# A sparse attention stage played from a written list instead of by due times, with three more score tiles and two more probability tiles

## The chip, the core and the metric

The kernel runs on one core of a Trainium2 chip. The metric is the device time of one execution in microseconds: 1283.05 us, the median of 3 runs (1282.41 to 1285.9). The engines are TensorE (PE in the profile; its weight loads are PEld), VectorE (DVE), ScalarE (ACT), GpSimd (POOL) and SyncE (SP), which only issues transfers. Each engine takes its own instructions in order and waits on semaphores for the others.

## What is computed

A convolution and pooling block, then a two-layer transformer on 256 tokens of width 1024, everything in float32. The first layer's mixer is a sparse attention with 16 query heads of 64 on 4 key/value heads, and this is the stage that the change rewrites:

```python
q, kc, vc, ks, vs, kw, vw, gates = split(h @ w_in)
kc = rmsnorm(compress_blocks(kc)); vc = compress_blocks(vc)     # 15 blocks: gelu(block @ w1) @ w2
ks, kw = rmsnorm(ks), rmsnorm(kw)
o_cmp = softmax(q @ kc, alibi, causal) @ vc
o_sel = softmax(q @ ks[selected], alibi, causal) @ vs           # at 256 tokens every block is selected
o_win = softmax(q @ kw, alibi, window) @ vw
o = g0 * o_cmp + g1 * o_sel + g2 * o_win
x = x + o @ w_out
```

Around it lie feed-forward layers (1024 to 2 x 2816 to 1024) and, later, a differential attention layer.

## The kernel before

Activations lie transposed, 128 features on partitions by 256 tokens. A float32 product is made of three fast products: each weight block is split into a rounded part `hi` (ScalarE, line 161) and a rest `lo` (VectorE, line 166), the activations likewise, and `mm3` (line 189) adds hi x hi, hi x lo and lo x hi. Weight blocks of 1 MB come through a ring of 4 `raw` tiles; `hi` and `lo` have 3 tiles each, so a block can be split only when a tile of an earlier block has been read for the last time. `Stream.prep` makes the two halves of each split as separate pieces of work, two blocks ahead. A `raw` tile is free when its `lo` is made, and SyncE then issues the next load.

The sparse stage (`nsa`, line 1035) runs from 430.3 to 596.8 us. Its parts, with the names of the changed text:

- `kc`, `vc`: 48 matmuls of 256 columns each; `post_c` (line 1062) scales them into `c2` (part of the big tile `nsaA`) and GpSimd's queue copies rows between partition halves; `fill_kcp` (F) adds the positions, `w1_q` multiplies with the two halves of the hidden layer (`hid`), `gelu`, `hid_t`, `ktilde_a`, `ktilde_b` (E0 to E3) make the compressed keys and values.
- Four projections of 48 matmuls with 512 columns: `nk`, `nq0`, `nv`, `nq1`, each 8 quanta of 6 matmuls; `norm_tok` (line 921) follows with a square and sum, a chain of twelve small VectorE operations (`factors`), a scaling, and two groups of four transposes (K, Z, N). `gt` is the gate projection, 24 matmuls.
- 16 pair units (4 head groups g, 2 branches b, 2 pairs i), each of seven steps. S: scores of two heads, 8 matmul records on 64 rows each, so that the two heads use different halves of the array. M: bias and running maximum (VectorE). X: exponential (ScalarE). G: reciprocal, gate and scaling (VectorE). T and U: three transposes each, of the first and the second head, and a copy (ScalarE). V: the product with the values, 8 records on 64 columns each, the two heads again on different halves. S takes both PSUM banks `s`, T one bank `pt`, U one bank `ptb`.
- Per group the compressed branch: a and b (softmax), c (transposes), e (product), and v, the evacuation of the group's output `O` into `oh` and `ol`.
- The output projection: 16 quanta of 12 matmuls of 256 columns, `q41` to `q52` and `y0` to `y3` in the new text; `post_res` adds to x and splits x anew (R), `squares` makes the norm's sums (Q).

Up to now the stage gives each piece of work a place in the program with `step`, `run` and `weave`; the units go in with `pipeline` as urgent background. A planner orders each engine's instructions by priority and by when it thinks an operand is ready, so instructions of several steps can mix on an engine. `in_order(True)` (line 339) makes TensorE, VectorE and ScalarE keep the order of the text, as is already done in the differential layer from 970.7 us on. The `P` tiles that hold scores are 5 in all, the `PT` tiles that hold transposed probabilities 3.

Of the kernel before, what the change touches and what calls it, by code (L numbers as in the profile page):

```python
# [17 lines left out]
T = 256  # L18
# [31 lines left out]
ET = mybir.EngineType  # L50
MAN = {ET.PE, ET.DVE, ET.Activation}

ADA_AT = {("win", 6): [(0, 8, 1)], ("win", 7): [(0, 9, 0)], ("win", 8): [(0, 10, 0)], ("win", 10): [(0, 11, 0), (1, 0, 1)],
# [118 lines left out]


PHASES = ("first", 0, "nsa", 1, 2, "diff", 3)


@with_exitstack
def body(ctx: ExitStack, tc, d, out, phases=PHASES):
# [139 lines left out]
    LA = 2  # L318
# [28 lines left out]
    def step(key, quanta, post, pre=(), extra_bg=(), keep=False):  # L347

        i = sid[key] if key is not None else None
        preps = st.prep(st.ahead(i, LA)) if i is not None else ([], [])  # L350
        pend = list(state["pend"])
        extra_bg = [urgent(f) for f in extra_bg]
        run(quanta, pre, weave(preps, pend + list(extra_bg)))
        state["pend"] = list(post)
# [599 lines left out]

        return [a, b, c, e(0), e(1)]

    def tr_unit(u, bank=None):
        def f():
            p = p_pt("PT") if bank is None else bank
            for i in range(3):  # L960
                PE.transpose(p[:, i * 128:(i + 1) * 128], u["s"][:, i * 128:(i + 1) * 128], C("ident"))
            s_ = sb.tile([128, 384], F32, tag="PT", name="PTs", bufs=3)

            A.copy(s_, p[:, 0:384])
            u["pt"] = s_
        return f
# [68 lines left out]
    def nsa():  # L1035
# [131 lines left out]

        def q_dst(g):
            return lambda p: A.copy(qhat[g], p)

        def group(key, post, ahead=False, bg0=(), bg1=()):
            pv = [pmm(key + "0"), pmm(key + "1")]
            step((key, 0), tok_quanta(pv, (key, 0), 0, ahead), [], extra_bg=bg0)
            step((key, 1), tok_quanta(pv, (key, 1), 1), post(pv), extra_bg=bg1)

        def post_v(pv):
            def f():
# [25 lines left out]
        dl = []  # L1203
        def post_nk(pv):
            f = norm_tok(pv, None, [k_dst(0), k_dst(1)], "nk")
            dl.extend(f[3:])
            return f[:3]
        group("nk", post_nk)
        step(("gt",), [gt_q], [post_gt, post_gt2])
        step(("w1", 1), w1_q(0), dl)  # L1210
        group("nq0", lambda pv: norm_tok(pv, C("invs")[:, 0:8], [q_dst(0), q_dst(1)], "nq0"))
        step(("w1", 3), w1_q(1), [gelu, hid_t, ktilde_a, ktilde_b])
        group("nv", post_v)

        obank = {}

# [4 lines left out]
        def cmp_units(g):  # L1221
# [45 lines left out]

            return b, b1, b2, c, e

        def pair_unit(g, i, b, cmp_b):  # L1270

            us = [{}, {}]
            slopes = [NSLOPE[(2 * i + n) * 4 + g] for n in range(2)]
            W = (slice(0, 128), slice(128, 384))
            c0 = 16 if b == 0 else 0
            WS = ((0, 128 + c0), (128 + c0, 384 + 2 * c0))
            kk = ksel if b == 0 else kwin
            qo = i * 256

            def S():  # L1280
                for u in us:
                    u["p"] = p_s("S")
                for t_, (s0, s1) in enumerate(WS):
                    for n, u in enumerate(us):
                        pa = slice(n * 64, n * 64 + 64)
                        mm(u["p"][:, s0:s1], qhat[g][pa, qo + t_ * 128:qo + (t_ + 1) * 128],
                           kk[pa, i, 0:s1 - s0], True, True)

            def M():
                mx = tiny("mx", 4)  # L1290
                nb = C("nbias")
                if b == 0:
                    if i == 0:
                        cell["sc", g] = cmp_b(us)
                    cb = C("cbias").rearrange("p (t n) -> p t n", t=2)
                    for n, u in enumerate(us):
                        V.tensor_tensor(cell["sc", g][:, :, 2 * i + n],
                                        u["p"][:, 0:288].rearrange("p (t n) -> p t n", t=2)[:, :, 0:15], cb, op=ALU.add)
                for n, u in enumerate(us):
                    u["s"] = sb.tile([128, 384], F32, tag="P", name="P", bufs=5)  # L1300
                    for t_, w in enumerate(W):
                        ws = slice(WS[t_][0] + c0, WS[t_][1])
                        V.tensor_tensor_reduce(out=u["s"][:, w], in0=u["p"][:, ws], in1=nb[:, w], scale=1.0,
                                               scalar=-3e38, op0=ALU.add, op1=ALU.max,
                                               accum_out=mx[:, 2 * n + t_:2 * n + t_ + 1])
                nm_ = tiny("nm", 4)
                o = (g * 2 + i) * 4
                V.tensor_tensor(nm_, mx, C("nsl4")[:, o:o + 4], op=ALU.mult)
                us[0]["nm"] = nm_

            def X():
                l = tiny("l", 4)
                for n, u in enumerate(us):
                    for t_, w in enumerate(W):
                        q = 2 * n + t_
                        A.activation(u["s"][:, w], u["s"][:, w], AF.Exp, bias=us[0]["nm"][:, q:q + 1],
                                     scale=slopes[n], accum_out=l[:, q:q + 1])
                us[0]["l"] = l

            def G():  # L1320
                rc = tiny("rc", 4)
                V.reciprocal(rc, us[0]["l"])
                rv = rc.rearrange("p (n t) -> p n t", n=2)
                gv = gts.rearrange("p (t kv g b) -> p kv t g b", t=2, kv=4, g=4)[:, 2 * i:2 * i + 2, :, g, 1 + b]
                V.tensor_tensor(rv, rv, gv, op=ALU.mult)
                for n, u in enumerate(us):
                    for t_, w in enumerate(W):
                        V.tensor_scalar(u["s"][:, w], u["s"][:, w], rc[:, 2 * n + t_:2 * n + t_ + 1], None, op0=ALU.mult)

            def Tr():  # L1330
                if "ptb" not in cell:
                    cell["ptb"] = pmm("ptb")
                for u, bank in zip(us, (None, cell["ptb"])):
                    tr_unit(u, bank)()

            def Av():
                if i == 0 and b == 0:
                    obank[g] = p_o("O")
                o = obank[g]
                vo = b * 256 + i * 128  # L1340
                for kb in range(2):
                    for n, u in enumerate(us):
                        mm(o[n * 64:(n + 1) * 64, i * 256 + kb * 128:(i + 1) * 256],
                           vv[:, kb * 512 + vo + n * 64:kb * 512 + vo + (n + 1) * 64],
                           u["pt"][:, 0:256] if kb == 0 else u["pt"][:, 256:384],
                           i == 0 and b == 0 and kb == 0, kb == 1)

            return {"S": S, "M": M, "X": X, "G": G, "T": Tr, "V": Av}

        def evac(g):  # L1350
            def f():
# [8 lines left out]
        seq = {g: [] for g in range(4)}  # L1360
        mark = {}
        for s_, sl in enumerate(slots):
            g, r = s_ // 4, s_ % 4
            lst = seq[min(g, 3)]
            lst += sl
            if g < 4 and r == 1:
                lst.append(cmps[g][1])
            elif g < 4 and r == 2:
                lst += [cmps[g][2], cmps[g][3]]
            if r == 2 and g >= 1:  # L1370
                lst += [cmps[g - 1][4], evac(g - 1)]
                mark.setdefault(g, len(lst))
        group("nq1", lambda pv: norm_tok(pv, C("invs")[:, 8:16], [q_dst(2), q_dst(3)], "nq1"),
              bg0=seq[0][:len(seq[0]) // 2], bg1=seq[0][len(seq[0]) // 2:])
        pend_, state["pend"] = state["pend"], []
        run([], (), weave(([], pend_), seq[1]))
        cut = mark[3]
        c_ = range(3)
        out_proj("no", oh, ol, P("ffn2")[:, 0:8],
                 [([(j, 0) for j in c_], 1, seq[2], ()), ([(j, 1) for j in c_], 2, seq[3][:cut], ()),  # L1380
                  ([(j, 2) for j in c_], 3, seq[3][cut:], ()), ([(0, 3)], 0, (), (0,)), ([(1, 3)], 4, (), (1,)),
                  ([(2, 3)], 0, (), (2,)), ([(3, ch) for ch in range(4)], 5, (), (3,))])


    def diff():
# [385 lines left out]
```

## Time and profile before

| | |
|---|---|
| median of 3 runs | 1283.05 us |
| profiled execution | 1282.53 us, its span 1280.8 us |
| TensorE busy | 1248.5 us, 97% |
| VectorE, ScalarE busy | 944.1 us (74%), 688.0 us (54%) |
| sparse stage | 430.3 to 596.8 us |

The profile is read from the chain that ended last to the stages: where the chain stays on TensorE with pieces of full length, the stage is bound there; where it jumps between engines every microsecond, something else sets the pace. A matmul's busy time holds its latency too (a 256-column matmul shows 0.28 us, though 48 follow one another in 5.70 us), so distances between starts are read here, not busy sums. A name like O<-PTs,nsaA says that tile O is written from tiles PTs and nsaA.

### The profile page before, as it was taken

The page shows a single profiled execution, that of the slowest core. Times are in us where ns is not written, and L with a number is a line of the kernel's source. Part 1 is how long each engine was busy: PE and PEld are TensorE (multiplying, and loading weights), DVE is VectorE, ACT ScalarE, POOL GpSimd, SP SyncE. Part 2 cuts the span into 40 slices and gives each one's busy share as a digit, 9 for nine tenths or more (in the row PEclk, how much of TensorE's full clock was granted, in tenths as well). Part 3 has the DMA queues.
Part 4 walks back from the last instruction along what each step waited for, and adds up shares of the span by engine and source line. Part 5 has one row for each costly group of instructions (what it writes and reads, how often), then busy time and mean ns, then how long its engine had stood idle before and what let it go on. Part 6 is the DMA issues. An engine that isn't in the chain of part 4 may idle for free.

```text
span 1280.8 us, 19880 instructions
## 1 busy us (share of the span) xinstructions
PE 1248.5 (97%) x7698; PEld 1081.5 (84%) x7698; DVE 944.1 (74%) x2005; ACT 688.0 (54%) x1284; POOL 4.2 (0%) x18
## 2 busy tenths in 40 slices
PE   5999999999999999999999999999999999999998
PEld 4998899788888976668888889888888779888888
DVE  6998796687766677777778656778656786887752
ACT  3455544566554346565655545655545676656631
POOL 0000000000000000000000000000000000000000
PEclk9999999899999999999999999999999999999999
DMA  8988676255555463104555555555554424555560
GB/s 307 379 314 328 226 278 215 101 197 198 173 177 201 165 241 131 64 34 141 188 184 178 178 191 193 195 178 177 180 191 163 165 99 165 182 186 192 181 198 17
DMA packets 34995, 238.61 MB, mean 186 GB/s; under 512 B 4050, under 2 KB 4178, under 8 KB 11220
## 3 DMA queue, kind: packets, MB, share of 16 engines
q1 hardware_dynamic: 34708, 236.82, 53.0%
q8 instruction: 60, 0.98, 0.3%
q0 software_dynamic: 192, 0.52, 0.2%
q14 instruction: 35, 0.29, 0.1%
HBM read 235.75 MB, written 1.05 MB: 185 GB/s over the span
## 4 chain that ended last, share of the span: by engine, by line
PE 89%; DVE 6%; DMA 2%; ACT 2%; issue 1%; SPq 0%; ACTq 0%; DVEq 0%
PE fin L187 38%; PE fout L187 19%; PE win L187 8%; PE y L187 3%; PE dqk L187 3%; PE op L187 3%; DVE lo L166 3%; PE S L187 2%; PE dv L187 2%; PE O L187 2%; DVE regA L508 1%; PE nq L187 1%; PE yT L187 1%; PE ad L187 1%; PE ssq L187 1%
## 5 line engine op out<-in xcount | busy, mean ns | idle before, releaser
L166 DVE TENSOR_TENSOR lo<-raw,hi 128x1024 fp32r<-128x1024 f32 (+2 forms) x404 | 471.0, 1182 | 152.9 <-ACT hi L161 152.6
L161 ACT CAST hi<-raw 128x1024 fp32r<-128x1024 f32 (+2 forms) x404 | 400.1, 1016 | 210.1 <-issue 119.3
L187 PE MATMUL fin<-xhl,hi 128*128 128x512 f32 x1408 | 495.4, 394 | 1.2 <-DVE x L988 0.6
L187 PE MATMUL fin<-xhl,lo 128*128 128x256 f32 x1408 | 398.6, 283 | 0.0
L187 PEld LDWEIGHTS fin<-xhl,hi 128*128 128x128 f32 x1408 | 264.3, 188 | 62.5 <-DVE x L988 1.3
L187 PEld LDWEIGHTS fin<-xhl,lo 128*128 128x128 f32 x1408 | 264.7, 188 | 0.3
L187 PE MATMUL fout<-gB,hi 128*128 128x512 f32 (+1 forms) x440 | 124.7, 349 | 0.0
L187 PE MATMUL fout<-gA,hi 128*128 128x512 f32 (+1 forms) x440 | 124.7, 349 | 0.0
L829 ACT ACTIVATE si<-ab 128x256 f32<-128x256 f32 x88 | 36.7, 419 | 140.9 <-DVE ab L824 140.9
L187 PE MATMUL win<-xhl,hi 128*128 128x256 f32 x576 | 105.1, 284 | 1.5 <-ACT xhl L522 1.5
L187 PE MATMUL fout<-gA,lo 128*128 128x256 f32 x352 | 99.4, 283 | 0.0
L187 PE MATMUL fout<-gB,lo 128*128 128x256 f32 x352 | 99.4, 282 | 0.0
L187 PEld LDWEIGHTS win<-xhl,hi 128*128 128x128 f32 x576 | 88.9, 188 | 2.6 <-ACT xhl L522 1.6
L187 PEld LDWEIGHTS fout<-gA,hi 128*128 128x128 f32 x440 | 76.6, 188 | 11.6
L187 PEld LDWEIGHTS fout<-gB,hi 128*128 128x128 f32 x440 | 76.6, 188 | 11.5
L822 ACT COPY ab<-fin 128x256 f32<-128x256 f32 x176 | 64.4, 369 | 34.9 <-PE fin L187 34.7
L187 PE MATMUL win<-xhl,lo 128*128 128x256 f32 x288 | 81.2, 283 | 0.0
L823 DVE TENSOR_TENSOR ab<-fin,ab 128x256 f32<-128x256 f32 x176 | 67.0, 418 | 3.1 <-ACT ab L822 3.1
L834 DVE TENSOR_TENSOR g<-si,ab 128x256 f32<-128x256 f32 x88 | 37.2, 425 | 41.5 <-ACT si L829 41.2
L187 PEld LDWEIGHTS fout<-gB,lo 128*128 128x128 f32 x352 | 66.2, 188 | 0.0
L187 PEld LDWEIGHTS fout<-gA,lo 128*128 128x128 f32 x352 | 66.2, 188 | 0.0
L824 DVE TENSOR_TENSOR ab<-ab,rB 128x512 f32<-128x512 f32 x88 | 60.0, 684 | 0.0
(410 smaller groups left out, 1634.6 us busy)
## 6 DMA issues: line engine op xcount, KB each, us to landing
raw<-in_fin_dram SPq DMA_DIRECT2D x88, 1024.0 KB, 4.9
raw<-in_fout_dram SPq DMA_DIRECT2D x32, 896.0 KB, 4.6
raw<-in_ada_dram SPq DMA_DIRECT2D x18, 1024.0 KB, 6.6
raw<-in_win_dram SPq DMA_DIRECT2D x18, 1024.0 KB, 6.3
raw<-in_fout_dram SPq DMA_DIRECT2D x16, 1024.0 KB, 4.9
raw<-in_wout_dram SPq DMA_DIRECT2D x8, 1024.0 KB, 6.5
raw<-in_d_qk_dram SPq DMA_DIRECT2D x8, 1024.0 KB, 4.8
raw<-in_wk_dram SPq DMA_DIRECT2D x8, 768.0 KB, 7.0
```

Source lines behind the costliest of these rows:

```text
L161: nc.scalar.copy(self.hl[i][0][:, sl], self.raw[i][:, sl])
L166: nc.vector.tensor_tensor(l[:, sl], self.raw[i][:, sl], h[:, sl].bitcast(F32), op=ALU.subtract)
L187: PE.matmul(o, lhsT, rhs, start=start, stop=stop, skip_group_check=True)
L508: V.tensor_tensor_reduce(out=scr, in0=r[:, i * 1024:(i + 1) * 1024], in1=cact, scale=1.0, scalar=0.0, op0=ALU.mult, op1=ALU.add, accum_out ...
L822: A.copy(t_[:, w], pt[i][:, 256:512])
L823: V.tensor_tensor(t_[:, w], pt[i][:, 0:256], t_[:, w], op=ALU.add)
L824: V.tensor_tensor(two(t_), two(t_), rb2(), op=ALU.mult)
L829: A.activation(s_, cell["t"][:, 0:256], AF.Silu)
L834: V.tensor_tensor(g, cell["s"], cell["t"][:, 256:512], op=ALU.mult)
```

## The change

The stage after `vc` runs under `in_order(True)` and is played from a written list, `NORD`: 253 names, each one step or one quantum with the splits (`hi`) that go with it. Each engine keeps that order, so the records of one S, T, U or V follow one another. The list also moves things: `fill_kcp` goes from the end of `vc` into the list (F0, F1); the window branch (b = 1) comes before the selected one, so that the first scores don't need the compressed keys; S0 comes when five of the eight `nv` quanta are done; the fourth output block takes its first three chunks as `q50` to `q52`. Three score tiles and two probability tiles are added in the part of `nsaA` where `c2` lay (`ring`). T and U become separate steps. No arithmetic is added or taken away.

```diff
+NORD = """
+C0 q0 q1 q2 l0 q3 l1 q4 l4 q8 g0 q6 F0 q5 l5 q7 g1 K0 K1 q9 q10 q11 K2 q12 q13 l8 q14 q15 q16 q19 F1 l13 q20 q17
+l14 l17 q18 l18 K3 q21 q22 q23 Z0 q24 q25 Z1 q27 q28 q31 E0 Z2 E1 Z3 E2 K4 E3 q26 S0 M0 q29 S1 l25 q30 M1 X0 l26
+S2 q32 M2 X1 G0 W S3 M3 X2 G2 Z4 q33 q34 T0 U0 a0 G1 S4 T1 M4 X4 l29 q35 U1 T2 S5 q36 b0 q37 M5 X5 q39 l30 G4
+q38 q40 l33 G5 V0 V1 X3 G3 N0 N1 U2 T3 S6 M6 U3 T4 N2 V2 V3 X6 c0 l34 S7 M7 N3 e0 v0 X7 a1 U4 T5 S8 M8 q41 G6
+q42 X8 S9 U5 l37 T6 M9 G7 b1 V4 V5 X9 U6 T7 S10 l38 M10 U7 c1 G8 V6 V7 S11 M11 N4 e1 G9 v1 T8 U8 X10 X11 S12 q43
+M12 q44 S13 T9 U9 V8 X12 V9 a2 G10 T10 U10 M13 G11 S14 G12 b2 M14 T11 U11 X13 V10 V11 c2 S15 G13 T12 M15 e2 l41
+l42 v2 U12 X15 X14 T13 q45 a3 q46 q47 q48 q49 G14 l44 l45 U13 T14 b3 V12 G15 c3 U14 l47 l48 V13 t0 T15 U15 t1 t4
+V14 V15 e3 t5 q50 v3 t2 t3 t6 y0 t7 R0 y1 Q0 y2 R1 R2 q51 q52 y3 Q1 Q2 R3 Q3
+"""
+NSPLIT = (2, 3, 4, 0, 0, 0)
...
+def play(order, acts):
+    order = order.split()
+    assert sorted(order) == sorted(acts), set(order) ^ set(acts)
+    for k in order:
+        for f in acts[k]:
+            f()
...
-        step(("vc",), pair_quanta(pt, ("vc",), X_H, X_L, range(8)), post_c(pt, 1) + [fill_kcp(0), fill_kcp(1)])
+        step(("vc",), pair_quanta(pt, ("vc",), X_H, X_L, range(8)), post_c(pt, 1))
...
+        turn = {}
+        def ring(nm, bufs, more, slot):
+            n = turn[nm] = turn.get(nm, -1) + 1
+            n = n % (bufs + more) - bufs
+            if n < 0:
+                return sb.tile([128, 384], F32, tag=nm, name=nm, bufs=bufs)
+            o = 2048 + (slot + n) * 384
+            return ra[:, o:o + 384]
...
-                    u["s"] = sb.tile([128, 384], F32, tag="P", name="P", bufs=5)
+                    u["s"] = ring("P", 5, 3, 0)
...
-            def Tr():
-                if "ptb" not in cell:
-                    cell["ptb"] = pmm("ptb")
-                for u, bank in zip(us, (None, cell["ptb"])):
-                    tr_unit(u, bank)()
+            def Tr(n):
+                def f():
+                    if n and "ptb" not in cell:
+                        cell["ptb"] = pmm("ptb")
+                    tr_unit(us[n], ring("PT", 3, 2, 3), cell["ptb"] if n else None)()
+                return f
...
-        units = [pair_unit(g, i, b, cmps[g][0]) for g in range(4) for b in range(2) for i in range(2)]
-        slots = pipeline(units, 1, 2, 3)
...
-        group("nq1", lambda pv: norm_tok(pv, C("invs")[:, 8:16], [q_dst(2), q_dst(3)], "nq1"),
-              bg0=seq[0][:len(seq[0]) // 2], bg1=seq[0][len(seq[0]) // 2:])
...
+        units = [pair_unit(g, i, b, cmps[g][0]) for g in range(4) for b in (1, 0) for i in range(2)]
...
+        def quarters(fs, preps):
+            hi, lo = preps
+            for j, f in enumerate(fs):
+                prods.append((f, hi[j::len(fs)], lo[j::len(fs)]))
...
+        for n, (f, hi, lo) in enumerate(prods):
+            acts[f"q{n}"] = [f] + hi
+            if lo:
+                acts[f"l{n}"] = lo
...
+        hi, lo = st.prep(st.ahead(sid["no", 4], 2))
+        for n, f in enumerate(hi + lo):
+            acts[f"t{n}"] = [f]
...
+        in_order(True)
+        play(NORD, acts)
+        state["pend"] = stats(2)
+        in_order(False)
```

So q0 to q7 are `nk`, q8 `gt`, q9 to q12 and q21 to q24 the hidden layer, q13 to q20 `nq0`, q25 to q32 `nv`, q33 to q40 `nq1`. C0 is `post_c` of `vc`, W the scaling of `nv`; l with a number is the `lo` of the split whose `hi` goes with the quantum of that number; t0 to t3 are the `hi` and t4 to t7 the `lo` of the next stage's first two blocks.

## Rows read from the trace of the kernel before

**Rows 1.** The page: busy time and share of the span, instructions of TensorE.
```profile
PE 1248.5 (97%) x7698; PEld 1081.5 (84%) x7698; DVE 944.1 (74%) x2005; ACT 688.0 (54%) x1284; POOL 4.2 (0%) x18
```

**Rows 2.** Windows: length, then busy us (instructions) by engine, PEclk, DMA share, GB/s.
```profile
442.96:493.57 50.61, 48.27 (x264) 37.02 (x264) 37.31 (x89) 19.82 (x30) 2.49 (x4) 1.00 0.61 217
493.57:596.82 103.25, 101.39 (x626) 70.57 (x626) 72.76 (x342) 66.25 (x198) 0.00 (x0) 1.00 0.19 66
970.67:1091.10 120.43, 117.58 (x692) 96.91 (x690) 93.16 (x280) 77.14 (x187) 0.00 (x0) 1.00 0.40 140
```

**Rows 3.** Chain that ended last: start us, us, engine, tile, records.
```profile
430.33 5.70 PE kc L187 x48
...
527.89 0.80 PE O L187 x8
...
552.20 0.90 PE S L187 x4
...
983.13 8.36 PE dv L187 x36
...
995.17 0.86 PE S L187 x8
...
1060.92 1.62 PE op L187 x12
```

**Rows 4.** Timeline of TensorE: start us, busy us, line, operation, tiles, records.
```profile
557.31 0.65 PE L187 MATMUL O<-PTs,nsaA 128*64 128x256 f32 x2
...
559.97 0.44 PE L961 MATMUL ptb<-cst,P 128*128 128x128 f32 x2
...
1065.15 0.49 PE L1478 MATMUL PT<-cst,P 128*128 128x128 f32 x3
1065.40 0.48 PE L187 MATMUL op<-difB,hi 128*128 128x256 f32 x2
```

**Rows 5.** Timeline of TensorE's weight loads: one of the two hidden-layer steps.
```profile
457.12 3.22 PEld L187 LDWEIGHTS hid<-raw,kcp 128*64 128x64 f32 x32
```

**Rows 6.** VectorE: a whole M, G, a chain alone, one mixed.
```profile
998.51 0.28 DVE L1445 CUSTOM_DVE_ANT_0 P<-S,cst 128x128 f32<-128x128 f32 x1
...
999.74 0.17 DVE L1448 TENSOR_SCALAR nm<-mx 128x4 f32<-128x4 f32 x1
...
519.02 1.00 DVE L1328 TENSOR_SCALAR P<-P,rc 128x128 f32<-128x128 f32 x4
...
462.84 0.18 DVE L403 TENSOR_TENSOR nka<-nkf 128x16 f32<-128x16 f32 x1
463.05 0.17 DVE L404 TENSOR_TENSOR nkb<-nka,nkv 128x16 f32<-128x16 f32 x1
...
522.28 0.17 DVE L409 SCALAR_TENSOR_TENSOR nq1f<-nq1b,nq1f 128x16 f32<-128x16 f32 x1
522.37 0.17 DVE L1322 RECIPROCAL rc<-l 128x4 f32<-128x4 f32 x1
```

**Rows 7.** Chain from 442 us: the stage's transfers.
```profile
447.55 6.13 DMA nsaA<-nsaA
...
461.86 6.96 DMA raw<-in_nv_dram
```

**Rows 8.** VectorE and ScalarE: a read beside a transfer, the end.
```profile
448.75 0.65 DVE L1085 TENSOR_TENSOR kcp<-nsaA,par 128x120 f32<-128x120 f32 x2 [0.76 <-DMA nsaA<-nsaA]
...
591.42 0.69 DVE L988 TENSOR_TENSOR x<-op,x 128x512 f32<-128x512 f32 x1
...
593.01 0.88 DVE L453 SCALAR_TENSOR_TENSOR xhl<-x,par,xhl 128x256 fp32r<-128x256 f32 x2
...
594.54 2.37 DVE L166 TENSOR_TENSOR lo<-raw,hi 128x1024 fp32r<-128x1024 f32 x2
...
593.48 1.99 ACT L161 CAST hi<-raw 128x1024 fp32r<-128x1024 f32 x2
```

More of the change, by code (lines that the diff above doesn't have):

```diff
@@ L955, in norm_tok, with tr_unit @@
         return [a, b, c, e(0), e(1)]
-    def tr_unit(u, bank=None):
+    def tr_unit(u, s_, bank=None):
         def f():
@@ L961, in f @@
                 PE.transpose(p[:, i * 128:(i + 1) * 128], u["s"][:, i * 128:(i + 1) * 128], C("ident"))
-            s_ = sb.tile([128, 384], F32, tag="PT", name="PTs", bufs=3)
             A.copy(s_, p[:, 0:384])
@@ L1169, in q_dst @@
             return lambda p: A.copy(qhat[g], p)
[L1171 to L1174, printed above, removed]
         def post_v(pv):
@@ L1201, in post_gt2 @@
             V.tensor_scalar(gts, gts, 0.5, 0.5, op0=ALU.mult, op1=ALU.add)
[L1203 to L1213, printed above, removed]
         obank = {}
@@ L1328, in G @@
                         V.tensor_scalar(u["s"][:, w], u["s"][:, w], rc[:, 2 * n + t_:2 * n + t_ + 1], None, op0=ALU.mult)
-            def Tr():
-                if "ptb" not in cell:
-                    cell["ptb"] = pmm("ptb")
-                for u, bank in zip(us, (None, cell["ptb"])):
-                    tr_unit(u, bank)()
+            def Tr(n):
[4 more added lines that the diff above has]
+                return f
             def Av():
-                if i == 0 and b == 0:
+                if i == 0 and b == 1:
                     obank[g] = p_o("O")
@@ L1345, in Av @@
                            u["pt"][:, 0:256] if kb == 0 else u["pt"][:, 256:384],
-                           i == 0 and b == 0 and kb == 0, kb == 1)
-            return {"S": S, "M": M, "X": X, "G": G, "T": Tr, "V": Av}
+                           i == 0 and b == 1 and kb == 0, kb == 1)
+            return {"S": S, "M": M, "X": X, "G": G, "T": [Tr(0), Tr(1)], "V": Av}
         def evac(g):
@@ L1357, in nsa @@
         cmps = [cmp_units(g) for g in range(4)]
-        units = [pair_unit(g, i, b, cmps[g][0]) for g in range(4) for b in range(2) for i in range(2)]
-        slots = pipeline(units, 1, 2, 3)
[L1360 to L1372, printed above, removed]
@@ L1373, in nsa @@
-        group("nq1", lambda pv: norm_tok(pv, C("invs")[:, 8:16], [q_dst(2), q_dst(3)], "nq1"),
-              bg0=seq[0][:len(seq[0]) // 2], bg1=seq[0][len(seq[0]) // 2:])
[L1375 to L1382, printed above, removed]
+        units = [pair_unit(g, i, b, cmps[g][0]) for g in range(4) for b in (1, 0) for i in range(2)]
@@ new lines, in nsa @@
+        prods = []
+        def quarters(fs, preps):
+            hi, lo = preps
+            for j, f in enumerate(fs):
+                prods.append((f, hi[j::len(fs)], lo[j::len(fs)]))
+        post = {}
+        for nm in ("nk", "gt", "w1", "nq0", "w1b", "nv", "nq1"):
+            if nm == "gt":
+                quarters([gt_q], st.prep(st.ahead(sid["gt",], LA)))
+                continue
+            if nm[:2] == "w1":
+                quarters(w1_q(nm == "w1b"), ([], []))
+                continue
+            pv = []
+            for half in range(2):
+                fs = tok_quanta(pv, (nm, half), half)
+                if half == 0:
+                    fs[0] = lambda f=fs[0], pv=pv, nm=nm: (pv.extend([pmm(nm + "0"), pmm(nm + "1")]), f())
+                quarters(fs, st.prep(st.ahead(sid[nm, half], LA)))
+            if nm == "nv":
+                post[nm] = post_v(pv)
+            else:
+                mul, dst = {"nk": (None, [k_dst(0), k_dst(1)]), "nq0": (C("invs")[:, 0:8], [q_dst(0), q_dst(1)]),
+                            "nq1": (C("invs")[:, 8:16], [q_dst(2), q_dst(3)])}[nm]
+                post[nm] = norm_tok(pv, mul, dst, nm)
@@ new lines, in nsa, with oq, f @@
+        pts = [None] * 4
+        def oq(j, ch):
+            def f():
+                if pts[j] is None:
+                    pts[j] = pmm(f"op{j}")
+                h, l = st.hl[sid["no", 4 if j == 3 else ch]]
+                for k in (2 * ch, 2 * ch + 1):
+                    o = slice(k * 256, (k + 1) * 256)
+                    for m in range(2):
+                        c0 = k * 256 + m * 128 if j == 3 else (k % 2) * 768 + (2 * j + m) * 128
+                        mm3(pts[j][:, m * 256:(m + 1) * 256], h[:, c0:c0 + 128], l[:, c0:c0 + 128], oh[:, o], ol[:, o],
+                            k == 0 and m == 0, k == 7)
+            return f
@@ new lines, in nsa @@
+        for n, (ch, js) in enumerate(((0, (0, 1, 2)), (1, (0, 1, 2)), (2, (0, 1, 2)), (0, (3,)), (1, (3,)), (2, (3,)))):
+            quarters([oq(j, ch) for j in js], st.prep(sid["no", NSPLIT[n]]) if NSPLIT[n] else ([], []))
+        acts = {}
+        for nm, fs in (("E", [gelu, hid_t, ktilde_a, ktilde_b]), ("K", post["nk"]), ("Z", post["nq0"]), ("N", post["nq1"]),
+                       ("F", [fill_kcp(0), fill_kcp(1)]), ("g", [post_gt, post_gt2]), ("C", state["pend"])):
+            for n, f in enumerate(fs):
+                acts[f"{nm}{n}"] = [f]
@@ new lines, in nsa @@
+        state["pend"] = []
+        acts["W"] = post["nv"]
+        for n, (f, hi, lo) in enumerate(prods):
+            acts[f"q{n}"] = [f] + hi
+            if lo:
+                acts[f"l{n}"] = lo
+        for u, fs in enumerate(units):
+            for w in "SMXGTV":
+                if w == "T":
+                    acts[f"T{u}"], acts[f"U{u}"] = fs["T"][:1], fs["T"][1:]
+                else:
+                    acts[f"{w}{u}"] = [fs[w]]
+        for g, (_, b1, b2, c, e) in enumerate(cmps):
+            acts[f"a{g}"], acts[f"b{g}"], acts[f"c{g}"], acts[f"e{g}"] = [b1], [b2], [c], [e]
+            acts[f"v{g}"] = [evac(g)]
@@ L1385, in diff @@
+        hi, lo = st.prep(st.ahead(sid["no", 4], 2))
+        for n, f in enumerate(hi + lo):
+            acts[f"t{n}"] = [f]
+        for j in range(4):
+            acts[f"y{j}"] = [oq(j, 3)]
+            acts[f"R{j}"], acts[f"Q{j}"] = (lambda j=j: [f() for f in post_res(pts[j], j, P("ffn2")[:, 0:8])[:3]],), \
+                squares(j)
+        in_order(True)
+        play(NORD, acts)
+        state["pend"] = stats(2)
+        in_order(False)
     def diff():
```

## The prediction

> **What bounds the kernel now.** I read the page first: TensorE is busy 97% of the span [rows 1]. That number holds latencies and says little of a stage, so I went on to the chain that ended last. Outside the sparse stage it is TensorE in whole pieces; inside, from 442.96 us (the end of `vc`) to 596.82 us, it changes engine or tile nearly every microsecond. That stretch is 153.86 us long and is all that the list orders; the rest of the kernel I leave unchanged.
>
> The windows say who is short of time in it [rows 2]. TensorE's busy time leaves 4.2 us of 153.86 open (50.61 + 103.25 less 48.27 + 101.39). VectorE is busy 37.31 + 72.76 us and ScalarE 19.82 + 66.25, so neither sets the pace as the order stands. TensorE does, though not by useful work. In the timeline 7 of the 16 S come in pieces: a half of one S takes 0.90 us, as long as a whole one, 0.86, because the two heads lie on different rows of the array and run side by side only if they follow one another [rows 3]. Of the 16 V, 11 come in pieces: one ran from 557.31 to 559.97 us with four single transposes between its records, 2.66 us where a whole V takes 0.80 [rows 3, 4].
>
> **The change part by part: TensorE's work when each step is whole.**
> - Projections: 192 matmuls of 512 columns at 8.36 / 36 = 0.232 us: 44.6. Output projection and gate: 192 + 24 of 256 columns at 5.70 / 48 = 0.119: 25.7 [rows 3].
> - Hidden layer: 2 x 3.22 = 6.4 [rows 5].
> - S: 16 x 0.86 = 13.8. V: 16 x 0.80 = 12.8 [rows 3].
> - T and U: 32 x 0.25 (1065.15 to 1065.40) = 8.0; the other 36 transposes (K, Z, N, c, the hidden layer's, the gate's) at a third of it: 3.0 [rows 4]. Four e, each four records, priced like a V: 3.2. The ten small products in E2 and E3 like a transpose: 0.9.
> - Changes of kind: an output stretch of 12 matmuls between two whole S takes 1.62 us, not 12 x 0.119 = 1.43 [rows 3], so leaving one kind and entering another costs 0.19 / 2 = 0.095. The list has 76 places where TensorE changes its kind of work: 7.2.
>
> Sum: 118.4 + 7.2 = 125.6 us, so 28.2 us of the 153.86 are there to win. The old excess accounts for it roughly: 7 S at 1.80 - 0.86 are 6.6, 11 V at up to 2.66 - 0.80 less four transposes (0.33) are up to 16.8, and 4.2 is open.
>
> **What the fixed order takes back.** Four terms.
>
> (a) The head. Three transfers set it, and the list doesn't change them. GpSimd's row copies end at 447.55 + 6.13 = 453.68, F0 (with its two memsets on GpSimd) follows, so `q9` starts at about 457.3 as it does now at 457.12 [rows 5, 7]. SyncE's first `nv` load lands at 468.82 [rows 7]; its `hi` stands in ScalarE's queue behind `q13`, and K3 and Z0 wait behind it. `l8` now stands behind K0 to K2 on VectorE, of which K1 alone is twelve small ops in a chain, 12 x 0.21 = 2.5 us [rows 6], so the second `nv` block is loaded some 3 us later than now; its first user is `q31`, after 476 us by the sum, so this costs nothing while that cover of about 5 us holds, and a microsecond for each beyond. What costs is E1, Z3, E2, K4, E3 in a row, with no quantum between them: each waits for one small answer from VectorE or ScalarE. Five hand-overs at about one small op with its start, 0.3 us, nearest to the 0.21 us step of a chain [rows 6]: 1.5 us (ends 0 and 4). S0 then comes at about 486 us.
>
> (b) VectorE's pace after S0. TensorE's share there is 84 us by the prices above. VectorE's: 16 units at M 1.31 (998.51 to 999.74 and a start) and G 1.00 + 0.4: 43.4; the extra sums of the selected branch 1.9; a, b, c of four groups at 2.5, small ops at 0.21 to 0.28 each: 10; N 5.1; v 2.5; 18 `lo` pieces, ten at 2.37 / 2 and eight of three quarters that size: 18.9; R and Q, 4 x (0.69 + 0.88) + 3 x 0.69: 8.4. That is 90 us [rows 6, 8], 13 of them after the last V. The two engines are level, and VectorE starts 2.5 us later, because M0 stands behind E3's chain of a dozen small ops. Running both sums along the list, TensorE has to wait at T1 (for G1, 1.0 us), at S8 (for M7, 1.4), at S15 (for M14, 1.5) and at y0 (for v3, 1.0): 5 us (ends 0 and 11, VectorE 10% dearer). ScalarE, busy 66.25 of 103.25 us now [rows 2], has slack, but X15 and X14 in a row hold G14 back; `q45` to `q49`, 7 us of TensorE work, cover that.
>
> (c) The end. t2 (ScalarE) makes the `hi` of the second next block. At that point three blocks still need their `hi` tile: the third-chunk block that y0 to y2 read, the last one, and the one that t0 made. So t2 waits for y2, and t3, t6, t7 and, since R0 stands behind t7 on VectorE, all of R wait with it. After y2 TensorE has `q51`, `q52`, y3: 4.3 us. VectorE needs t6 and t7 (from 1.1 to 3.4 us after y2), then 2 us for each of R0 to R3 and Q between, casts on ScalarE included [rows 8]. The next stage's first block takes x in pieces of 0.7 us in the order in which R makes them; by that running sum it loses 0.9 + 0.6 + 0.6 + 2.0 = 4.1 us (ends 0 and 6).
>
> (d) Small waits that the sums don't see. The differential stage already runs in order; TensorE is idle there 120.43 - 117.58 = 2.85 us [rows 2]. For 126 us that is 3.0 (ends 2 and 6).
>
> The five extra tiles, the split of T and U and the window branch put first add no instruction; they only free M and T from waiting for earlier units, and I cost them at nothing. If that freedom weren't there, M would wait for a U two units back, which by the list is done before it nearly everywhere.
>
> Sum: 125.6 + 1.5 + 5 + 4.1 + 3.0 = 139.2 us, 14.7 less than now. The profiled execution took 1282.53 us, 0.5 below the median of the runs; 1282.53 - 14.7 + 0.5 = 1268.3 us.
>
> A rule that bears on (b): in a mixed order a small VectorE op starts 0.09 us after the one before (522.28, 522.37), in a chain alone 0.21 (462.84, 463.05) [rows 6]. [...]
>
> **The rivals.**
> - VectorE becomes the bound. For: 90 against 84 us, and the dearer chains. Against: 13 of the 90 come after the last V. With a tenth more on VectorE, (b) is 11 in place of 5 and (d) some more: 1275 us (1272 to 1280). Chance 0.20.
> - The covers hold: TensorE's queue is never behind VectorE's, and R runs ahead of the t pieces or the first block doesn't need it so early. (b) and (c) vanish: 1268.3 - 9.1 = 1259 us (1256 to 1263). Chance 0.15.
> - The list doesn't do what it says: broken steps were filler in time in which TensorE would have stood anyway, and whole steps turn into open waits. For: the planner put them where an operand was ready. Against: VectorE is idle 30 of 103.25 us in the second window [rows 2], so it isn't what TensorE would wait for. Then 1279 to 1286. Chance 0.05.
> - Slower: false waits on `nsaA`. The extra tiles lie inside the big tile that also holds keys and values, which every S and V reads. 24 tile writes (12 of M, 12 of T and U) go there. If a write waited for all earlier reads of the big tile and not of its own part, each would hold VectorE or ScalarE for a S and a V, 1.66 us: 40 us, 1308. It decides against the change from 14.7 / 24 = 0.6 us per write. Against: a read of one part of `nsaA` started at 448.75 us while a transfer into another part ran until 453.68 [rows 7, 8]. Chance 0.05.
>
> **How the numbers follow.** The forecast case (1263 to 1272 us) has 0.55. The likeliest time is 1268.3. The range reaches down into the second rival and up to the dear end of the first: 1259 to 1279, which leaves out about 0.2. Within 0.3% of now (3.8 us, about what a measurement of this kernel can tell from no change) is 0.06, from the third rival and the end of the first; slower by more 0.06; faster by more 0.88.
>
> **What the profile of after would show.** Right: S in 8 records of 0.86 and V in 8 of 0.80 nearly always; S0 at about 486 us; the next stage's first block at about 575 to 580 us with gaps in it behind R; VectorE over 85% busy from S0 on. Wrong: open waits of TensorE for VectorE of more than 10 us in sum (first rival), none at all (second), or waits of M and of the copies for V (last). S0 later than 490 us would mean that the head lost time to a transfer or to E.

## The result and the profile after

The changed kernel takes 1265.45 us (median of 4 runs, 1264.21 to 1266.22) against 1283.89 for the kernel before on the same chip: ratio 0.9852, 95% interval 0.9831 to 0.9873. The forecast was 1268.3 in a range of 1259 to 1279. Its profiled execution took 1264.76 us, with a span of 1263.0.

The page of after, engines with busy time, share and instructions; the same 7698 matmuls take 17.8 us less of TensorE [rows 1]:

```profile
PE 1230.7 (97%) x7698; PEld 1076.7 (85%) x7698; DVE 947.6 (75%) x2005; ACT 685.5 (54%) x1284; POOL 4.3 (0%) x18
```

Windows of after (columns as in rows 2): from the end of `vc` to the first S, from there to the next stage's first block, and the differential stage.

```profile
443.74:487.94 44.20, 43.76 (x243) 33.52 (x241) 31.81 (x80) 16.61 (x26) 2.64 (x6) 1.00 0.64 219
487.94:577.24 89.30, 86.93 (x647) 68.73 (x647) 79.65 (x347) 65.14 (x195) 0.00 (x0) 1.00 0.27 91
952.89:1073.30 120.41, 117.61 (x690) 96.88 (x689) 93.16 (x280) 77.01 (x186) 0.00 (x0) 1.00 0.40 140
```

The two windows that answer to 153.86 us of before are together 133.50 us long. TensorE leaves 0.44 and 2.37 us open in them. VectorE is busy 79.65 of 89.30 us, 89%, where it was 70% [rows 2]. The differential stage is as long as before to 0.02 us.

TensorE's timeline of after (start us, busy us, line, operation, tiles, matmul shape, records, wait in brackets):

```profile
516.35 0.43 PE L208 MATMUL O<-nsaA 128*64 128x256 f32 x1
...
516.95 0.92 PE L208 MATMUL O<-PT,nsaA 128*64 128x128 f32 x9
517.80 0.44 PE L1263 MATMUL pct<-cst,pcp 128*128 128x128 f32 x2
518.17 1.14 PE L208 MATMUL S<-nsaA,qhat 64*128 64x144 f32 x8
520.07 0.66 PE L971 MATMUL nq1T<-cst,nq1n 128*128 128x128 f32 x4 [0.76 <-DVE PCs L1265]
...
521.43 0.49 PE L982 MATMUL ptb<-cst,P 128*128 128x128 f32 x3
521.76 0.49 PE L982 MATMUL PT<-cst,P 128*128 128x128 f32 x3
522.18 0.98 PE L208 MATMUL S<-nsaA,qhat 64*128 64x128 f32 x8
523.08 0.50 PE L208 MATMUL op<-nsaB,hi 128*128 128x256 f32 x2
```

Two V, 16 records of O, run from 516.35 to 517.80: 0.73 us each. An S follows in eight records, and 0.90 us after 522.18 the next kind of work begins. All 16 S have their 8 records together; no V is broken.

TensorE's waits from 443 to 600 us (tile that waits <- what it waits for: us in total, times, longest):

```profile
PE fin L208 <- DVE xhl L474: 1.9, 2, 1.0
PE nq1T L971 <- DVE PCs L1265: 0.8, 1, 0.8
PE nq0T L971 <- DVE nq0n L961: 0.4, 2, 0.2
PE S L208 <- DVE mx L1318: 0.2, 1, 0.2
PE PT L982 <- DVE P L1343: 0.2, 1, 0.2
```

The end of the stage, in the chain that ended last (start us, us, engine, tile, records):

```profile
567.65 4.32 PE op L208 x34
...
572.00 1.06 ACT hi L173
...
573.08 2.36 DVE lo L178 x2
575.44 0.61 DVE x L1008
...
579.70 0.41 DVE xhl L474
...
580.15 8.39 PE fin L208 x46
```

A `hi` waits until y2 has read its tile, the `lo` pieces follow on VectorE, then R's first x and the split of it. The next stage's first block starts at 577.24 and stands once more until the second x is split (579.70 to 580.11).

### The profile page after: what moved, and what is told of

It reads as the page before. It is cut to its first block, busy times and chain, and to the rows that moved or that the text cites. A ratio compares the mean times of both kernels' runs of the same rounds, so it can differ in the third digit from the quotient of the medians.

```text
span 1263.0 us, 19864 instructions
## 1 busy us (share of the span) xinstructions
PE 1230.7 (97%) x7698; PEld 1076.7 (85%) x7698; DVE 947.6 (75%) x2005; ACT 685.5 (54%) x1284; POOL 4.3 (0%) x18
## 3 DMA queue, kind: packets, MB, share of 16 engines
HBM read 235.75 MB, written 1.05 MB: 187 GB/s over the span
## 4 chain that ended last, share of the span: by engine, by line
PE 52%; DVE 2%; ACT 1%; issue 0%; DVEq 0%; ACTq 0%
PE fin L208 29%; PE fout L208 15%; PE dqk L208 3%; PE dv L208 2%; PE op L208 2%; DVE lo L178 1%; PE S L208 0%; PE dO L208 0%; PE PT L1549 0%; DVE x L1008 0%; PE ssq L208 0%; ACT hi L173 0%; DVE P L1516 0%; DVE xhl L474 0%; PE OT L1593 0%
```

## The experiments

Whole times carry a disturbance that has nothing to do with the change: in the fourteen profiled executions the work ahead of the stage ended anywhere between 439.92 and 447.02 us, and from the first S of the differential layer to the end of the span all took 285.61 to 285.83 us. So I read each trace between two starts of TensorE records, the last matmul of `vc` and the first S of the differential layer, and split it in four: to the first S of the stage; on to the last matmul of the output projection; on to the next stage's first matmul; on to the differential S. The starts are read in each kernel's timeline; the differences are mine. Each row is one execution. The first column differs by 1.6 us (43.58 to 45.20) among the nine runs whose text is the same up to the first S, so a smaller difference there says nothing; the second differs by 0.1 us among the four whose work behind the first S is the same or as dear (after, after_again, e1, e4).

| kernel | median us | ratio to before, interval | to first S | to last output matmul | to next stage | to differential S | sum |
|---|---|---|---|---|---|---|---|
| before | 1283.89 | | 50.68 | 102.97 | 0.12 | 398.44 | 552.21 |
| after | 1265.45 | 0.9852 (0.9831 to 0.9873) | 44.32 | 88.14 | 1.17 | 400.07 | 533.70 |
| after_again | 1264.23 | 0.9847 (0.9831 to 0.9863) | 44.36 | 88.07 | 1.17 | 400.08 | 533.68 |
| e1_tail | 1262.82 | 0.9841 (0.9827 to 0.9856) | 44.07 | 88.16 | 0.12 | 398.61 | 530.96 |
| e2_tiles | 1282.67 | 0.9994 (0.9983 to 1.0006) | 52.41 | 101.64 | 0.12 | 398.44 | 552.61 |
| e3_planner | 1270.16 | 0.9906 (0.9889 to 0.9923) | 45.41 | 95.34 | 0.12 | 398.43 | 539.31 |
| e4_apart | 1264.84 | 0.9855 (0.9838 to 0.9871) | 44.60 | 88.14 | 1.18 | 400.08 | 533.99 |
| e5_broken | 1277.41 | 0.9957 (0.9943 to 0.9972) | 44.33 | 101.51 | 1.18 | 400.08 | 547.10 |
| e6_plain | 1277.26 | 0.9952 (0.9935 to 0.9969) | 53.75 | 92.19 | 0.12 | 398.44 | 544.50 |
| e7_best | 1261.07 | 0.9830 (0.9814 to 0.9845) | 43.66 | 89.28 | 0.12 | 398.61 | 531.66 |
| e8_twice | 1274.97 | 0.9944 (0.9928 to 0.9961) | 43.58 | 98.16 | 1.18 | 400.08 | 543.00 |
| e9_lessV | 1262.05 | 0.9831 (0.9816 to 0.9846) | 44.20 | 85.62 | 1.17 | 400.08 | 531.09 |
| e10_lessP | 1265.13 | 0.9858 (0.9840 to 0.9876) | 43.86 | 85.24 | 4.32 | 400.40 | 533.81 |
| e11_lessVP | 1263.38 | 0.9825 (0.9798 to 0.9852) | 45.20 | 81.90 | 4.32 | 401.39 | 532.81 |

**Are broken steps what cost the time? e5_broken** takes the changed kernel and breaks every S in two, the second head behind the next step of TensorE and M behind that. The work is the same; some M come later on VectorE.

```diff
-... S0 M0 q29 S1 l25 q30 M1 ...
+... S0 q29 s0 M0 S1 l25 q30 s1 M1 ...
```

> The changed kernel, with every S taken apart: the first head at S's place in the list, the second head behind the next step of TensorE (a quantum, a T, an N, a Z), and M behind that. Same work on every engine, only whole steps undone for S. By the rows a half of an S takes 0.90 us, so 16 S cost 16 x (1.80 - 0.86) = 15 us more of TensorE. Theory (TensorE's work sets the time after S0, VectorE nearly as late): 10 to 15 us more than the changed kernel, 1275 to 1280 us. Rival (broken steps are filler, TensorE has as much time to spare): up to 4 us more, below 1270 us.

Measured 1277.41 us; the sum is 13.40 us longer than after's, all of it between the first S and the last output matmul. TensorE's timeline of e5_broken:

```profile
508.62 0.92 PE L208 MATMUL S<-nsaA,qhat 64*128 64x128 f32 x4
509.47 0.73 PE L208 MATMUL nq<-hi,xhl 128*128 128x512 f32 x2
...
511.07 0.92 PE L208 MATMUL S<-nsaA,qhat 64*128 64x128 f32 x4
511.92 0.73 PE L208 MATMUL nq<-hi,xhl 128*128 128x512 f32 x2
```

The second window of e5_broken (in after TensorE is busy 86.93 us there):

```profile
487.39:590.08 102.69, 100.19 (x648) 75.11 (x647) 81.20 (x347) 65.75 (x195) 0.00 (x0) 1.00 0.23 79
```

TensorE's busy time grows by 13.26 us, so it is TensorE's time that the broken steps cost; its open time is 2.50 us, 2.37 in after. Half an S holds TensorE for 0.85 us (508.62 to 509.47, 511.07 to 511.92), as long as a whole one. By the timeline there are 29 runs of S records in place of 16 (three halves happen to meet the next S); 13 more at 0.85 are 11.1 us, and the rest lies within 13 more changes of kind and waits. Broken steps were no filler: the third rival falls.

**The tiles alone. e2_tiles** is the kernel before with the five extra tiles.

```diff
-            s_ = sb.tile([128, 384], F32, tag="PT", name="PTs", bufs=3)
...
-                    u["s"] = sb.tile([128, 384], F32, tag="P", name="P", bufs=5)
+                    u["s"] = ring("P", 5, 3, 0)
...
-                    tr_unit(u, bank)()
+                    tr_unit(u, ring("PT", 3, 2, 3), bank)()
```

> The kernel before, with the three score tiles and two probability tiles alone; the planner orders as before. Theory (tiles only free M and T from waiting, TensorE's broken steps stay): 1283 us, within 3 us of the kernel before. Rival (M and T wait for tiles in the kernel before and the tiles give part of the gain): 1275 us or less.

Measured no difference: 0.9994, and a sum 0.40 us longer. They were costed at nothing, and with the planner's order they are worth nothing; no run takes them out of the held order. It also speaks against false waits on `nsaA`: 24 tile writes a stage go there, and the stage is no longer for it.

**The list without holding the order. e3_planner** keeps the text of the list but lets the planner order the engines.

```diff
-        in_order(True)
         play(NORD, acts)
         state["pend"] = stats(2)
-        in_order(False)
```

> The changed kernel, with the list played in the same order but without holding the engines to it: the planner is free to mix steps. Theory (the gain is that S, T, U and V stay whole): S and V come in pieces again and most of the gain goes, 1277 to 1285 us. Rival (the gain is where the list puts things: window branch first, S0 before the end of nv, fillers between units): 1270 us or less.

The theory was wrong: 1270.16 us, at the edge of what the rival said. Its two windows:

```profile
439.92:485.33 45.41, 43.64 (x243) 33.68 (x242) 33.53 (x81) 16.95 (x26) 2.63 (x6) 1.00 0.66 233
485.33:580.79 95.46, 92.06 (x647) 68.92 (x647) 76.13 (x350) 68.03 (x201) 0.00 (x0) 1.00 0.22 75
```

With the text in the list's order the planner kept all 16 S whole of itself, though it broke V into 18 runs of records where after has 12. Against before the sum is 12.90 us shorter; holding the order then brings 5.61 more (539.31 to 533.70): 8.3 in the stage less 2.7 given back at its end, where e3 gives nothing back. So the larger part of the gain comes without `in_order`. It is not all due to where the text puts the steps: in the list the units also lose their urgent priority, which the next run takes away by itself.

**The old priority. e6_plain** is the kernel before with the units' pieces no longer urgent.

```diff
-        def g():
-            with tc.high_priority(URG):
-                f()
-        return g
+        return f
```

> The kernel before, with the urgency of the background pieces taken away, so that the planner orders S, T, V and the projections by their place in the program alone. Theory (pieces mix on TensorE because urgent units overtake one another and the quanta): fewer S and V in pieces, and some of the gain, 1272 to 1280 us. Rival (the mix comes from the planner choosing whatever is ready, urgent or not): as many pieces, 1280 to 1290 us.

Measured 1277.26 us, and the sum 7.71 us shorter than before. Its two windows:

```profile
441.68:495.43 53.75, 51.12 (x278) 39.32 (x276) 39.10 (x91) 22.65 (x33) 2.49 (x4) 1.00 0.58 211
495.43:587.74 92.31, 88.30 (x613) 63.81 (x613) 71.23 (x340) 62.28 (x194) 0.00 (x0) 1.00 0.20 69
```

Fewer S are broken (3 in place of 7), and after the first S it needs 92.19 us in place of 102.97; the first S comes 3 us later. Of the 18.5 us that the change brings, 7.7 could be had by dropping the priority alone: the urgent background tore four of the seven S. Which of its effects brings the time was not taken apart further. From e6 to e3 the sum falls by another 5.19 us (544.50 to 539.31), for the text's places together with the tiles and the split of T and U, and from e3 to the held order by 5.61. Taken in this order, none of the three steps alone makes half of the gain.

**Side by side, or only contiguous? e4_apart** writes the four products of one head first and then those of the other, within each S.

```diff
-                for t_, (s0, s1) in enumerate(WS):
-                    for n, u in enumerate(us):
+                for n, u in enumerate(us):
+                    for t_, (s0, s1) in enumerate(WS):
```

> The changed kernel, with the score products of each S sorted by head and not by block of queries: the same 8 records, but the two heads no longer alternate. Two S of the kernel before that came in this order took 1.42 us where an alternating one takes 0.86. Theory (TensorE's work sets the time after S0): 16 x 0.56 = 9 us more, less some 2 us that hide in waits for VectorE: 1271 to 1275 us. Rival (VectorE paces that stretch, or broken steps are filler): within 2 us of the changed kernel, 1264 to 1267 us.

The edit was to make S dearer and so test whether TensorE sets the pace. It did not make S dearer (1264.84 us), so it says nothing of that. TensorE's timeline of e4_apart:

```profile
522.74 0.98 PE L208 MATMUL S<-nsaA,qhat 64*128 64x128 f32 x8
523.65 0.50 PE L208 MATMUL op<-nsaB,hi 128*128 128x256 f32 x2
```

An S takes 0.91 us in this order too (0.90 in after). The records start in pairs 0.06 us apart as in after, though the program has the other head's first product four matmuls further on; the records don't name their head, so that a pair holds both is read from the equal shapes. It follows that the heads need not alternate in the text. That both stand in one uninterrupted run is needed (e5), but it isn't always enough. The S of before that took 1.42 us has its eight records together too, in TensorE's timeline of before:

```profile
496.21 1.49 PE L187 MATMUL S<-nsaA 64*128 64x144 f32 x8
497.63 0.73 PE L187 MATMUL nq<-hi,xhl 128*128 128x512 f32 x2
```

By the shapes the second head starts there only with the last record of the first, 0.55 us after it; its first weight load stands behind a semaphore wait of its own. What held it back was not tested. The Trainium skill (TensorEngine Tiling (Array Packing), Tiling Modes, Key Properties) says that different tiles of the array load and multiply in parallel and that a change of the tiling mode drains TensorE; the trace agrees with the first; the second has no run here that isolates it.

**The end. e1_tail** moves four splits of the next stage's blocks behind R2.

```diff
-V14 V15 e3 t5 q50 v3 t2 t3 t6 y0 t7 R0 y1 Q0 y2 R1 R2 q51 q52 y3 Q1 Q2 R3 Q3
+V14 V15 e3 t5 q50 v3 y0 R0 y1 Q0 y2 R1 R2 t2 t3 t6 t7 q51 q52 y3 Q1 Q2 R3 Q3
```

> The changed kernel, with t2, t3, t6, t7 moved behind R2 in the list, so that R0 to R2 no longer stand behind the splits that wait for y2. Theory (the end of the stage loses time because R stands behind them): the changed kernel shows 1.17 us of TensorE idle before the next stage's first block and 1.25 us inside it; both should go, R0 starts 2.9 us before y2 ends. Expected 2.0 us less than the changed kernel, 1263 to 1264 us. Rival (the planner of the next stage already fills that time with the second block, and the second block's splits now come later): no difference, 1265 us, or up to 1 us more, because the second block is then not there to fill.

Measured 1262.82 us; the sum is 2.74 us shorter, of which 1.05 lie before the next stage's first matmul and 1.46 behind it, 2.5 us in place of the 2.0 that the theory gave; the rest lies ahead of the first S, within its scatter. VectorE's timeline of e1_tail:

```profile
568.19 0.69 DVE L1008 TENSOR_TENSOR x<-op,x 128x512 f32<-128x512 f32 x1 [1.67 <-PE op L208]
569.46 0.89 DVE L474 SCALAR_TENSOR_TENSOR xhl<-x,par,xhl 128x256 fp32r<-128x256 f32 x2 [0.58 <-ACT xhl L470]
...
573.59 0.88 DVE L474 SCALAR_TENSOR_TENSOR xhl<-x,par,xhl 128x256 fp32r<-128x256 f32 x2 [0.58 <-ACT xhl L470]
574.92 2.36 DVE L178 TENSOR_TENSOR lo<-raw,hi 128x1024 fp32r<-128x1024 f32 x2 [0.45 <-ACT hi L173]
```

R's x and its splits now come first (568.19 to 574.5) and the `lo` pieces behind them; TensorE's two waits for `xhl` are gone from its waits.

**Is VectorE on the path? e8_twice** makes the `lo` of five output blocks twice, 9.5 us more for VectorE and nothing for the others.

```diff
+                    for _ in range(2 if i in self.twice else 1):
...
+        st.twice = {sid["no", i] for i in range(5)}
```

> The changed kernel, with the rest part (lo) of the five output projection blocks made twice on VectorE: ten more ops in the stretch after S0, 8 x 0.89 + 2 x 1.18 = 9.5 us. VectorE is busy 79.65 of the 89.30 us after S0 in the changed kernel. Theory (the two engines are level there): most of it shows, 5 to 9 us more, 1270 to 1274 us. Rival (TensorE alone sets the time and VectorE's 9.7 open us take the extra ops): less than 2 us more.

Measured 9.5 us more, and 10.02 in the stretch behind the first S. Its second window, and TensorE's waits in it:

```profile
486.89:586.22 99.33, 88.76 (x647) 69.19 (x647) 89.66 (x357) 65.30 (x195) 0.00 (x0) 1.00 0.24 82
```

```profile
PE op L210 <- DVE nsaB L1372: 4.4, 2, 2.6
PE S L210 <- DVE mx L1320: 1.9, 4, 0.7
...
PE pct L1265 <- DVE rc L1339: 1.6, 1, 1.6
```

All of the addition shows, a little more than the theory's 5 to 9 us. From the first S to v3, behind which these operations do not reach, VectorE has no slack to take them: in after it is busy 75.39 of the 78.98 us from 487.94 to 566.92.

**Is it alone on the path? e9_lessV** leaves out the scaling in G of every second head: 10.4 us by the operations' own times, which overlap on VectorE. **e10_lessP** leaves out the third product of the sparse output projection (the weights' rest with the rounded values): 7.6 us less for TensorE. **e11_lessVP** does both.

```diff
 e9                 for n, u in enumerate(us):
-                for n, u in enumerate(us):
+                for n, u in enumerate(us[:1]):
 e10
-                        mm3(pts[j][:, m * 256:(m + 1) * 256], h[:, c0:c0 + 128], l[:, c0:c0 + 128], oh[:, o], ol[:, o],
-                            k == 0 and m == 0, k == 7)
+                        mm(pts[j][:, m * 256:(m + 1) * 256], h[:, c0:c0 + 128], oh[:, o], k == 0 and m == 0, False)
+                        mm(pts[j][:, m * 256:(m + 1) * 256], h[:, c0:c0 + 128], ol[:, o], False, k == 7)
```

> The changed kernel once more, as the mark for the three runs beside it: 1265 us, ratio to the kernel before 0.985 to 0.987 by every theory.

> The changed kernel with the scaling of the second head's G left out in each of the 16 steps, so the division by the sum and the gate are missing for every second head: 16 operations of about 0.65 us, 10.4 us of VectorE's work less. Theory (TensorE and VectorE level behind S0): TensorE takes the end as soon as VectorE is shorter, 2 to 4 us are saved, 1261 to 1263. Rival (VectorE alone is the bound): 8 to 10 us saved, 1255 to 1257. Rival (TensorE alone): nothing, 1265.

> The changed kernel with the third of the three products of the sparse output projection left out (its low-order part of the values): 64 matmuls of 0.119 us, 7.6 us of TensorE's work less. Theory (level): 1 to 3 us saved, 1262 to 1264. Rival (VectorE alone is the bound): nothing, 1265. Rival (TensorE alone): 6 to 8 us saved, 1257 to 1259.

> Both omissions at once: 10.4 us less on VectorE and 7.6 us less on TensorE. Theory (level): far more than the two alone added up, 7 to 9 us saved, 1256 to 1258. Rival (one engine alone is the bound): what that engine's own omission saved and no more.

By whole times e9 came as the level theory has it (2.2 us less than after_again), while e10 (0.9 more) and e11 (0.9 less, with runs from 1257.42 to 1264.5) missed it. The second window of e9, e10 and e11 in this order, from the first S to the next stage's first matmul, and TensorE's waits of e10:

```profile
487.35:574.15 86.80, 85.66 (x647) 68.13 (x647) 73.12 (x315) 64.88 (x195) 0.00 (x0) 1.00 0.27 93
```

```profile
490.88:580.43 89.55, 80.23 (x583) 61.38 (x583) 81.79 (x349) 67.03 (x197) 0.00 (x0) 1.00 0.28 98
```

```profile
489.21:575.43 86.22, 79.27 (x583) 60.66 (x583) 75.18 (x317) 66.83 (x197) 0.00 (x0) 1.00 0.29 101
```

```profile
PE fin L208 <- DVE xhl L474: 4.0, 1, 4.0
PE pct L1263 <- DVE rc L1337: 1.5, 1, 1.5
PE op L208 <- DVE nsaB L1370: 1.3, 2, 0.7
```

The columns of the table part what the whole time mixes. Between the first S and the last output matmul, 88.07 us in after_again, e9 saves 2.45, e10 2.83 and e11 6.17. By the windows VectorE's busy time falls by 6.5 us in e9 (79.65 in after, 73.12) and TensorE's by 6.7 in e10 (86.93, 80.23). So each brings some two fifths of what was taken away, and both together more than the two added up: there the engines are level. But e10 and e11 lose it at once: TensorE now waits 4.0 us for the first split of x. ScalarE's timeline of e11:

```profile
568.59 2.00 ACT L173 CAST hi<-raw 128x1024 fp32r<-128x1024 f32 x2 [3.82 <-PE op L208]
571.43 1.99 ACT L173 CAST hi<-raw 128x1024 fp32r<-128x1024 f32 x2 [0.85 <-PE op L208]
573.33 0.90 ACT L470 ACTIVATE xhl<-x,par 128x256 fp32r<-128x256 f32 x2
```

The y quanta are shorter, so fewer matmuls lie behind y2, and two more `hi` pieces (571.43) stand ahead of R's first cast (573.33) than in after, where it follows the first two. e11 gives back 3.15 us before the next stage and 1.31 in it. The wait at the end grows when TensorE gets faster.

**Two more moves in the list. e7_best** is e1_tail with `q26` put between Z2 and E1 and N3 behind U4.

```diff
-... E0 Z2 E1 Z3 E2 K4 E3 q26 S0 ...
+... E0 Z2 q26 E1 Z3 E2 K4 E3 S0 ...
-... S7 M7 N3 e0 v0 X7 a1 U4 T5 S8 ...
+... S7 M7 U4 N3 e0 v0 X7 a1 T5 S8 ...
```

> The changed kernel with three moves in the list: t2, t3, t6, t7 behind R2 (as in the run on the end of the stage), q26 between Z2 and E1 in place of behind E3, and N3 behind U4 in place of before e0. In the changed kernel TensorE waits 0.35 + 0.40 us at Z3, 0.20 at E1 and 0.83 us at N3. Theory (these waits are on the path): 1 to 1.7 us less than with the moved t pieces alone. Rival (VectorE is as late, and a wait taken from TensorE comes back at the next T or S): no difference from the moved t pieces alone.

Measured 1261.07 us, the lowest median, but its interval and e1_tail's overlap, and by the table the two added moves bring 0.41 us ahead of the first S, within the scatter of that column, and cost 1.12 behind it. What makes both kernels shorter than after is e1's move.

## Why the prediction was right, and where its terms were not

The forecast's sign, mechanism and size hold: 18.4 us came where 14.7 were forecast, and 1265.45 lies in the forecast case's own 1263 to 1272. From the end of `vc`, the stretch and what is lost behind it are 133.50 + 400.07 - 398.44 = 135.1 us; the sum was 139.2. Its terms:

- **Whole steps free TensorE: right.** S and V run whole, and e5 shows the price by undoing it: 0.85 us for each half. To put the gain down to the fixed order as a whole was too coarse: 12.9 us come without holding the order (e3), and of these 7.7 can be had from dropping the old priority alone (e6).
- **TensorE's work, 125.6 us: too small.** The window shows 130.69 busy. That figure holds some latency, so it is an upper bound, and it also hides waits: e9, with the same work for TensorE, shows 85.66 us busy behind the first S in place of 86.93. Rows carry part of the difference: T and U follow one another after 0.33 us (521.43 to 521.76), where I took 0.25, and an S comes after 0.42 (522.18), where I took 0.345 with the change of kind, which over 32 of them is some 2.6 us. An S with no wait takes 0.86 to 0.92 us, as I had it, and two V in a row 0.73 each in place of 0.80. If the whole excess over 118.4 were put to the 76 changes of kind, each would cost (130.69 - 118.4) / 76 = 0.16 us in place of 0.095. No run isolates it.
- **(a) The head: nearly right.** The first S came 44.20 us after `vc`, at 487.94; 43.0 were forecast. TensorE shows busy for 43.76 of the 44.20, and the list of waits has 0.4 us for `nq0n`, but the 1.2 us are less than this stretch differs between executions (1.6), and how they divide into work and waits stays open.
- **(b) VectorE's pace: mechanism right, waits mis-sized.** I had 77 us of VectorE's work up to the last V (90 less 13); the trace shows 75.39 us busy up to v3. e8 shows VectorE full, e9 to e11 that the two are level. The waits came to 1.2 us by the profile's list (nq1T 0.8, S 0.2, PT 0.2), and e9, which takes VectorE's load away, wins 2.45 in all: half of the 5 I forecast. The longest in the list is none of the four that I named: it is N3 at 520.07, which stands behind VectorE's copy PCs. Of the four, T1 shows 0.2 us, S8 and y0 none in the list, and S15 more than the list counts:

```profile
548.74 1.52 PE L208 MATMUL S<-nsaA,qhat 64*128 64x144 f32 x8 [0.25 <-DVE mx L1318]
```

S15 stands 0.25 us ahead of its first head and again inside, for the second: the next step starts at 550.19, 1.45 us after it in place of some 0.90. Why the waits came out at half is not shown; a running sum with too little work for TensorE lets it arrive too early at every wait, which fits, but no run tests that.
- **(c) The end: right place, smaller.** t2 waits for y2 and R for the splits, as told; e1 shows the price by removing it, 2.5 us in place of 4.1. Part is covered because TensorE, while the second x isn't split, goes on at 578.24 with further matmuls of the next stage, which I had not allowed for; which block they belong to and what the cover is worth is not shown.
- **(d) Small waits, 3.0 us: too much.** All that TensorE leaves open in the stretch is 133.50 - 130.69 = 2.8 us, of which about 1.0 is the first wait for `xhl`, so (a), (b) and (d) together show 1.8 in place of 9.5.

So the error has parts that half cancel: 5.1 us too little for TensorE's busy time, some 1.3 of them hidden waits by e9, against 7.7 us too many open waits and 1.4 too much at the end (1.0 + 1.63 in place of 4.1). That makes the 4.0 us by which the sum was too long (139.2 - 135.1 = 4.1), and that the total came so near is in part luck.

**The rivals.** VectorE as the only bound falls with e9. Covers that hold are the nearest miss in waits, but the end's cost is there. Broken steps as filler falls with e5, false waits with e2 and with the result itself. The dearer chains are there: in the held order a dependent pair of small operations starts 0.20 us apart, as VectorE's timeline of after shows,

```profile
508.49 0.17 DVE L1337 RECIPROCAL rc<-l 128x4 f32<-128x4 f32 x1
508.69 0.17 DVE L1340 TENSOR_TENSOR rc<-rc,nsaA 128x4 f32<-128x4 f32 x1
```

against 0.09 us for two of different chains in the mixed order [rows 6]. The Trainium skill (VectorE: DVE Perf Modes, The DRAIN you can't avoid) says that the next operation waits until the pipe is empty, and that one that is not held starts earlier; the pair 0.09 us apart, each busy 0.17, agrees with the second. Keeping steps together made VectorE's load only a little larger: 111.46 us busy in the stretch against 110.07 [rows 2].

## What to carry to other kernels

Where two half-array steps overlap only if they stand together, count broken pairs in the timeline before anything else: each cost a whole step here (0.85 us), and a background priority can be what breaks them. A run that leaves out a priority and moves the text at once does not say which of the two brought the time. When two engines come out level in the sum, test with both loads, added and taken away, because taking away from one shows only a part; and take the size of a load from the engine's busy time in the window, not from the sum of overlapping operations. Compare stretches between two fixed records of the trace, not whole times alone, and look at the hand-over behind the stage, where a gain can be given back.

## What the runs showed of the hardware that was not expected

- Two heads' matmuls on different rows of the array start 0.06 us apart even where the program puts four matmuls of one head before the first of the other (e4_apart: 0.91 us for an S against 0.90); in before an S whose records also stand together took 1.42 us.
- The time at which the work ahead of the stage ends differs by up to 7.1 us between executions (439.92 to 447.02), although that part of the program is nearly the same in all; the part behind the stage repeats to 0.2 us.
